# A two-layer hybrid-attention decoder: stick-breaking gates under their own units, the stick-breaking output projection under the softmax units, a later rotary factor, fewer gates at the end of attention

## The chip, the cores and the metric

The kernel runs on one core of a Trainium2 chip. The metric is the device time of one execution in microseconds (us). The engines are named as in the profile: PE (TensorE, matrix products), PEld (its weight loads), DVE (VectorE), ACT (ScalarE), POOL (GpSimd) and SP (SyncE, which issues most DMAs). Each engine works through its own instructions in order.

## The reference

Two layers over x of 512 rows and 1024 columns, all in float32:

```
h  = rms_norm(x, g_attn);  proj = h @ w_in              # 1024 -> 5120 columns
dq, dk, dv, sq, sk, sv, gates = split(proj)             # 6 x 512 columns and 2 x 1024
dq, dk = rope(dq), rope(dk)
o_diff = (softmax(q1 k1') - lam * softmax(q2 k2')) v    # 4 heads, then rms_norm over 128
o_sb:  a[i,j] = sigmoid(z[i,j]) * prod over j < t < i of sigmoid(-z[i,t]);  o = a v   # 8 heads of 64
g_diff, g_sb = split(sigmoid(gates + b_gate))
x = x + (g_diff * (o_diff @ w_o_diff) + g_sb * (o_sb @ w_o_sb)) @ w_out
x = x + (silu(gate) * up) @ w_ffn_out                   # gate, up = split(rms_norm(x, g_ffn) @ w_ffn_in)
```

and a last rms_norm. Hidden width of the FFN: 2816.

## The kernel before

Everything is kept transposed: a tile has 128 channels as partitions and the 512 rows of x as columns. Every large product is made of three matmuls: each float32 operand is split into a high part and a low part, and `mm_tiles` issues high x high, low x high and high x low for each of the eight (or four) blocks of 128 channels (lines 259 to 261). A group of 128 output channels is thus 24 matmuls of 128x512, or 12 where only half of the channels enter.

Weights come as a stream whose order is a list (`layer_order`). `w_pieces` allocates for entry n a raw buffer `wr` (three of them), a high part `wh` and a low part `wl` (four each), issues the DMA on SP, the cast `wr` to `wh` on ACT (L127) and the subtraction that gives `wl` on DVE, or on POOL for every fourth entry of w_in (L129). `w_get` hands the parts to the product and keeps the stream two entries ahead.

Attention has eight units: s0 to s3 are pairs of stick-breaking heads (class `SB`), d0 to d3 the softmax heads (class `Diff`). Each needs three groups of w_in (key, query, value). An SB unit makes scores, sigmoid (ACT, L504/506), a reverse scan (DVE), a product with the scan (POOL, L511), transposes on PE (L488), their high and low parts (`ths` on ACT L491, `tls` on DVE L492), and the map times values (`avs`, L522/523). A Diff unit makes scores, maxima, exponentials, a mix of two maps, transposes, `avd` (L576 to 578), squares `osd` and their parts `ohd`, `old` (L583 to 588), their mean `omd` on PE (L589/590), Ln and Exp (`rsqrt_of`, L206/207), three steps on DVE and the scaled output `od` (L592).

The order of the work on PE is set by a list of slots: while unit n runs, `fill` issues the three groups of unit n+1 and, from the fifth slot on, groups of gates (`FILL` is three groups in slots 0 to 3, four in 4 to 7). The 16 gates of a layer are w_in's groups 24 to 39, 24 to 31 for the softmax branch (`gd`) and 32 to 39 for the stick-breaking one (`gs`). Nine of them are left for the end (`TAIL0`). A gate's bank is multiplied by the norm's factor r on DVE; its sigmoid waits until the last Exp (`state["exp"]`), since ACT has to load another table for it. After attention, `parts` splits the eight unit outputs (L637); for each of the eight groups m of w_o, `ws` (stick-breaking half) and `wd` (softmax half) follow, then two sigmoids (L655, L656), three DVE operations that merge, and the split of the result. Then come the output projection `wo` and the FFN.

At the start of a layer the two halves of the rotary table `cs` are multiplied by r (L355, L356), ahead of the first evictions of unit s0 (`kns`, `qns`, `vns`, L397). `vns` feeds the transposes `vts` on PE (L450). `table()` loads the ACT tables: sigmoid for the SB units, Ln and Exp behind their last sigmoid.

The code before is written in program order; the framework's scheduler then orders each engine's instructions.

Of the kernel before, what the change touches and what calls it, by code (L numbers as in the profile page):

```python
# [34 lines left out]
BUFS = dict(mx=4, sm=4, blk=12, tmp=5, stk=6, v=3, wk=4, wT=3)  # L35
BANK_BUFS = dict(mm=3, at=5)
W_BUFS, W_AHEAD = 4, 2
GATES_IN_BLK = 4
# [6 lines left out]
FILL = (3, 3, 3, 3, 4, 4, 4, 4)  # L45
# [8 lines left out]
def trunk(ctx: ExitStack, tc, xT, par, tab, scn, msk, w_in, w_o, w_out, w_fi, w_fo, out):  # L54
# [17 lines left out]
    GATES = []  # L72
    for m in range(8):
        GATES += [("in", 24 + 8 + m), ("in", 24 + m)]
    layer_order = list(unit_groups(UNITS[0]))
    slots = []
    gi = 0
    for n in range(8):
        g = unit_groups(UNITS[n + 1]) if n < 7 else []
        while len(g) < FILL[n] and gi < len(GATES):  # L80
            g.append(GATES[gi])
            gi += 1
        slots.append(g)
# [28 lines left out]
    def w_pieces(*steps):  # L112
# [5 lines left out]
        raw = wp.tile([P, 1024], F32, name=f"wr{n}", tag="wr", bufs=3)  # L118
# [4 lines left out]
        for n_cols in steps:  # L123
# [4 lines left out]
            eng = nc.gpsimd if stream[n][1] == "in" and n % 4 == 0 else nc.vector  # L128
# [3 lines left out]
    def w_sums():  # L132
# [5 lines left out]
        pool, tag, bufs = (wp, "wr", 3) if j % 2 else (fp, "wx", 2)  # L138
# [133 lines left out]
    nrm = Norm(C_NA, "a0")  # L272
    pieces = [w_pieces(128, 384, 512), w_pieces(512, 512), w_pieces(1024)]
# [54 lines left out]
    for l in range(DEPTH):  # L328
        h = nrm.h
        with ExitStack() as ac:  # L330
# [24 lines left out]
            nc.vector.tensor_tensor(out=cs[:, 0], in0=cs[:, 0], in1=r, op=ALU.mult)  # L355
            nc.vector.tensor_tensor(out=cs[:, 1], in0=cs[:, 1], in1=r, op=ALU.mult)  # L356
# [8 lines left out]
            pair = [None]  # L365
            TAIL = list(TAIL0)

            def gate_group(key):
# [3 lines left out]
                n = len(gates)  # L372
                if n < GATES_IN_BLK:
                    t = blk(f"gt{j}")
                elif n < GATES_IN_BLK + BUFS["stk"]:
                    t = T("stk", f"gt{j}")
                elif n < GATES_IN_BLK + BUFS["stk"] + 2:
                    t = T(f"klz0{n - GATES_IN_BLK - BUFS['stk']}", f"gt{j}")
                else:
                    q = (n - GATES_IN_BLK - BUFS["stk"]) % 2  # L380
                    if q == 0:
                        pair[0] = T("wk", f"gt{j}", (P, 1280))
                    t = pair[0][:, q * S:q * S + S]
# [112 lines left out]
            class SB(Unit):  # L496
                def maps(self, c):
# [7 lines left out]
                    for i, (o, n) in enumerate(BANKS):  # L505
# [3 lines left out]
                    nc.vector.tensor_tensor_scan(out=e[:, ::-1], data0=e[:, ::-1], data1=msc[:, ::-1], initial=1.0,  # L509
                                                 op0=ALU.mult, op1=ALU.max)  # L510
# [3 lines left out]
                def mix(self, c, a):  # L514
# [9 lines left out]
                    if c == 0:  # L524
                        self.o = blk("o" + self.n)
# [11 lines left out]
            class Diff(Unit):  # L537
# [25 lines left out]
                def mix(self, m1, m2):  # L563
# [15 lines left out]
                    self.o = blk("o" + self.n)  # L579
# [27 lines left out]
            def fill(key):  # L607
                n = sum(u.done == 3 for u in units)
# [5 lines left out]
            for i in range(16 + LAG):  # L614
# [21 lines left out]
            def parts(t, hi, lo):  # L636
# [268 lines left out]
```

## Time and profile before

| | |
|---|---|
| median of 3 runs | 1497.26 us (1497.13 to 1498.28) |
| the profiled execution | 1496.57 us |
| its span | 1494.8 us |
| PE busy | 1461.4 us, 98% |
| DVE, ACT, POOL busy | 976.0, 691.8, 483.0 us |
| mean granted clock of PE | 0.995 |

The span is the time from the first to the last instruction in the trace; the time of an execution is a little longer. Busy time is summed by engine; engines run side by side. Matmul instructions overlap in the trace, so the distance of two starts and not the duration of one is what a matmul takes. A row of a timeline reads: start, duration, engine, line, operation, output<-inputs, shape, and in brackets the idle time just before with what ended it. Layer 0's attention lies at about 35 to 285 us, layer 1's at about 775 to 1030.

### The profile page before, as it was taken

How to read it: one execution, taken by the hardware profiler on the slowest of the kernel's cores; microseconds unless marked ns; L12 is line 12 of the kernel's file. 1: busy time of each engine (PE TensorE's matmuls, PEld its weight loads, DVE VectorE, ACT ScalarE, POOL GpSimd, SP SyncE). 2: the span in 40 equal slices, each digit the busy share in tenths (PEclk: the TensorE clock that was granted, in tenths of full speed). 3: DMA queues.
4: the chain of work that ended last, by engine and by line, in shares of the span. 5: the costliest groups of instructions: out<-in, count | busy, mean ns of one | idle time of the engine just before them, and what ended most of it. 6: DMA issues, size and time to landing. Idle time of an engine off the chain costs nothing.

```text
span 1494.8 us, 19780 instructions
## 1 busy us (share of the span) xinstructions
PE 1461.4 (98%) x7670; PEld 1253.0 (84%) x7670; DVE 976.0 (65%) x1229; ACT 691.8 (46%) x1122; POOL 483.0 (32%) x317
## 2 busy tenths in 40 slices
PE   9899999999999999999998999999999999999996
PEld 7788888888888998998886878888888989989885
DVE  6978776475765757654658777765648467477544
ACT  5656554643642433433444645546336334335342
POOL 2454652001140723530224455510022226155112
PEclk9999999999999999999999999999999999999998
DMA  7122232132323323223421122322323233232232
GB/s 254 46 78 69 75 102 86 57 124 94 106 96 103 108 87 105 90 83 87 134 85 57 64 75 88 100 81 80 103 94 117 90 99 113 74 124 71 87 88 66
DMA packets 45934, 139.73 MB, mean 93 GB/s; under 512 B 5904, under 2 KB 8336, under 8 KB 45840
## 3 DMA queue, kind: packets, MB, share of 16 engines
q1 hardware_dynamic: 45120, 137.91, 28.7%
q8 instruction: 60, 0.98, 0.3%
q10 hardware_dynamic: 720, 0.56, 0.1%
q14 instruction: 34, 0.28, 0.1%
HBM read 132.16 MB, written 2.10 MB: 90 GB/s over the span
## 4 chain that ended last, share of the span: by engine, by line
PE 87%; DVE 6%; ACT 3%; issue 1%; POOL 1%; DMA 1%; SPq 0%; DVEq 0%; POOLq 0%; ACTq 0%
PE fa L725 8%; PE fc L725 4%; PE pg L259 4%; PE pg L260 4%; PE pg L261 4%; PE fo L259 3%; PE fo L260 3%; PE fo L261 3%; PE fg L259 3%; PE fg L260 3%; PE fu L261 3%; PE fg L261 3%; PE fu L260 3%; PE fu L259 3%; PE fb L725 2%; PE wo L259 2%
## 5 line engine op out<-in xcount | busy, mean ns | idle before, releaser
L127 ACT CAST wh<-wr 128x1024 fp32r<-128x1024 f32 (+4 forms) x223 | 213.8, 964 | 327.5 <-issue 55.3
L129 DVE TENSOR_TENSOR wl<-wr,wh 128x1024 fp32r<-128x1024 f32 (+3 forms) x201 | 247.6, 1236 | 77.4 <-ACT wh L127 75.9
L259 PE MATMUL pg<-hha,wh 128*128 128x512 f32 x256 | 101.0, 394 | 0.0
L261 PE MATMUL pg<-hla,wh 128*128 128x512 f32 x256 | 100.3, 392 | 0.0
L260 PE MATMUL pg<-hha,wl 128*128 128x512 f32 x256 | 100.1, 391 | 0.0
L129 POOL TENSOR_TENSOR wl<-wr,wh 128x1024 fp32r<-128x1024 f32 (+3 forms) x22 | 50.7, 2305 | 111.8 <-ACT wh L127 99.2
L706 POOL TENSOR_TENSOR p<-u,g 128x512 f32<-128x512 f32 x22 | 34.4, 1563 | 158.0 <-DVE u L763 154.5
L242 POOL TENSOR_TENSOR accf<-accf,sqf 128x512 f32<-128x512 f32 x10 | 18.5, 1846 | 199.9 <-ACT sqf L240 199.9
L259 PE MATMUL fo<-ah,wh 128*128 128x512 f32 (+1 forms) x220 | 82.8, 376 | 0.0
L260 PE MATMUL fo<-ah,wl 128*128 128x512 f32 (+1 forms) x220 | 82.6, 375 | 0.0
L261 PE MATMUL fo<-al,wh 128*128 128x512 f32 (+1 forms) x220 | 82.3, 376 | 0.0
L259 PE MATMUL pd<-hha,wh 128*128 128x512 f32 x192 | 76.4, 398 | 0.3 <-ACT knd3s L404 0.3
L260 PE MATMUL pd<-hha,wl 128*128 128x512 f32 x192 | 76.2, 397 | 0.0
L261 PE MATMUL pd<-hla,wh 128*128 128x512 f32 x192 | 76.0, 396 | 0.0
L144 POOL TENSOR_TENSOR tf<-ru,rg 128x512 f32<-128x512 f32 x22 | 31.8, 1446 | 128.5 <-DMA ru<-in_w_fi_dram 112.3
L259 PE MATMUL fg<-hhf,wh 128*128 128x512 f32 x176 | 69.1, 393 | 0.0
L260 PE MATMUL fg<-hhf,wl 128*128 128x512 f32 x176 | 69.1, 393 | 0.0
L261 PE MATMUL fu<-hlf,wh 128*128 128x512 f32 x176 | 68.7, 390 | 0.0
L261 PE MATMUL fg<-hlf,wh 128*128 128x512 f32 x176 | 68.7, 390 | 0.0
L260 PE MATMUL fu<-hhf,wl 128*128 128x512 f32 x176 | 68.6, 390 | 0.0
L259 PE MATMUL fu<-hhf,wh 128*128 128x512 f32 x176 | 68.6, 390 | 0.0
L259 PE MATMUL ps<-hha,wh 128*128 128x512 f32 x144 | 58.8, 409 | 0.0
(452 smaller groups left out, 4492.0 us busy)
## 6 DMA issues: line engine op xcount, KB each, us to landing
wr<-in_w_in_dram SPq DMA_DIRECT2D x78, 512.0 KB, 3.3
wr<-in_w_fi_dram SPq DMA_DIRECT2D x44, 512.0 KB, 3.3
wr<-in_w_fo_dram SPq DMA_DIRECT2D x32, 384.0 KB, 3.1
rg<-in_w_fi_dram SPq DMA_DIRECT2D x22, 512.0 KB, 3.3
ru<-in_w_fi_dram SPq DMA_DIRECT2D x22, 512.0 KB, 3.3
wr<-in_w_fo_dram SPq DMA_DIRECT2D x32, 320.0 KB, 2.9
wr<-in_w_o_dram SPq DMA_DIRECT2D x16, 512.0 KB, 3.3
wr<-in_w_out_dram SPq DMA_DIRECT2D x16, 512.0 KB, 3.3
```

The costliest lines, as they stand in the source:

```text
L127: nc.scalar.copy(out=hi[:, c], in_=raw[:, c])
L129: state["wl"] = eng.tensor_tensor(out=lo[:, c], in0=raw[:, c], in1=f32(hi[:, c]), op=ALU.subtract)
L144: tt = lambda eng, o, a, b: eng.tensor_tensor(out=o, in0=a, in1=b, op=ALU.subtract)
L242: eng.tensor_tensor(out=self.acc, in0=self.acc, in1=sq, op=ALU.add)
L259: nc.tensor.matmul(dst, hi[:, c], rh, start=first and k == 0, stop=False)
L260: nc.tensor.matmul(dst, lo[:, c], rh, start=False, stop=False)
L261: nc.tensor.matmul(dst, hi[:, c], rl, start=False, stop=last and k == n - 1)
L706: (nc.vector if u.space == bass.MemoryType.PSUM else nc.gpsimd).tensor_tensor(out=p, in0=u, in1=g, op=ALU.mult)
L725: nc.tensor.matmul(dst, x[:, c], y, start=first and k + n == 0, stop=n == 2 and k == len(a) - 1, skip_group_check=True)
```

## The change

- Gates of the stick-breaking branch (`GS`): two in each of slots 0 to 3. They have buffers of their own (tag `gs`), and their sigmoids follow at once, with the table that the SB units use.
- Gates of the softmax branch (`GD`): one in slot 4, three in slot 7, four in the tail. Their eight sigmoids still wait for the last Exp.
- w_o is streamed in halves, `os` (stick-breaking) and `od` (softmax), 16 entries of 512 columns instead of 8 of 1024. The `os` groups run in slots 5 and 6, two in each, and four in the tail; `ws` times gate is formed there. The outputs of the SB units are split inside the units.
- After the last unit only the `od` groups are left, m = 0 and 1 first over the first three units.
- The two multiplications of `cs` come after the fourth scan.
- Raw weight buffers: two instead of three, and one of its own for the first entry. POOL no longer makes the low part of the entries 0, 4 and 132.

```diff
-GATES_IN_BLK = 4
-FILL = (3, 3, 3, 3, 4, 4, 4, 4)
...
+    GD, GS = [("in", 24 + m) for m in range(8)], [("in", 32 + m) for m in range(8)]
+    OS = [("os", m) for m in range(8)]
+    slots = [GS[0:2], GS[2:4], GS[4:6], GS[6:8], GD[0:1], OS[0:2], OS[2:4], GD[1:4]]
+    for n in range(7):
+        slots[n] = slots[n] + unit_groups(UNITS[n + 1]) if n == 3 else unit_groups(UNITS[n + 1]) + slots[n]
+    TAIL0 = [GD[4], OS[4], GD[5], GD[6], OS[5], GD[7], OS[6], OS[7]]
...
-    layer_order += [("o", m) for m in range(8)] + [("out", m) for m in range(8)]
+    layer_order += [("od", m) for m in range(8)] + [("out", m) for m in range(8)]
...
+        if kind in ("od", "os"):
+            return w_o[l, i][:, 512 * (kind == "os"):][:, :512]
...
-        raw = wp.tile([P, 1024], F32, name=f"wr{n}", tag="wr", bufs=3)
+        if n:
+            raw = wp.tile([P, 1024], F32, name=f"wr{n}", tag="wr", bufs=2)
+        else:
+            raw = state["w0"].tile([P, 1024], F32, name="wr0")
...
-            eng = nc.gpsimd if stream[n][1] == "in" and n % 4 == 0 else nc.vector
+            eng = nc.gpsimd if stream[n][1] == "in" and n % 4 == 0 and n % len(layer_order) > 6 else nc.vector
...
-            nc.vector.tensor_tensor(out=cs[:, 0], in0=cs[:, 0], in1=r, op=ALU.mult)
-            nc.vector.tensor_tensor(out=cs[:, 1], in0=cs[:, 1], in1=r, op=ALU.mult)
...
+            def os_group(m):
+
+                b = bank("mm", f"ws{m}_{l}")
+                hi, lo = w_get(l, "os", m)
+                mm_tiles(b, hi, lo, os_, True, True)
+                nc.vector.tensor_tensor(out=gates[8 + m], in0=b, in1=gates[8 + m], op=ALU.mult)
...
                 gates[j] = t
+                if j >= 8:
+                    bias = pt[:, C_BG + 16 * l + j:C_BG + 16 * l + j + 1]
+                    sigs.append(nc.scalar.activation(out=t, in_=t, func=AF.Sigmoid, bias=bias))
...
+                    if c == 1:
+                        os_.append(parts(self.o, T("osp", "oh" + self.n, dt=F32R), T("osp", "ol" + self.n, dt=F32R)))
...
+                    if i == 3:
+                        with tc.issue_after(state["z"].ins):
+                            for a in range(2):
+                                nc.vector.tensor_tensor(out=cs[:, a], in0=cs[:, a], in1=r, op=ALU.mult)
                     if i == 7:
-                        state["tab"] = table(LNEXP, state["sig"])
+                        with ExitStack() as order:
+                            for s in sigs:
+                                order.enter_context(tc.issue_after(s.ins))
+                            state["tab"] = table(LNEXP, state["sig"])
...
+            for u in units[4:]:
+                od_.append(parts(u.o, hp.tile([P, S], F32R, name=f"oh{u.n}_{l}", tag="hh"),
+                                 hp.tile([P, S], F32R, name=f"ol{u.n}_{l}", tag="hl")))
             merged = []
+
+            wd = [(fbank(f"wd{m}_{l}"),) + w_get(l, "od", m) for m in range(2)]
+            for b, hi, lo in wd:
+                mm_tiles(b, hi, lo, od_[:3], True, False)
             for m in range(8):
-                hi, lo = w_get(l, "o", m)
-                bs, bd = fbank(f"ws{m}_{l}"), fbank(f"wd{m}_{l}")
-                mm_tiles(bs, hi, lo, os_, True, True, 4)
-                mm_tiles(bd, hi, lo, od_, True, True, 0)
+                if m < 2:
+                    bd, hi, lo = wd[m]
+                    mm_tiles(bd, hi, lo, od_[3:], False, True, 3)
+                else:
+                    bd = fbank(f"wd{m}_{l}")
+                    mm(bd, (l, "od", m), od_)
...
                 with tc.issue_after(state["exp"].ins):
-                    nc.scalar.activation(out=gs, in_=gs, func=AF.Sigmoid, bias=pt[:, bg + 8 + m:bg + 9 + m])
                     sig = nc.scalar.activation(out=gd, in_=gd, func=AF.Sigmoid, bias=pt[:, bg + m:bg + 1 + m])
-                nc.vector.tensor_tensor(out=gs, in0=bs, in1=gs, op=ALU.mult)
                 nc.vector.tensor_tensor(out=gd, in0=bd, in1=gd, op=ALU.mult)
                 nc.vector.tensor_tensor(out=gd, in0=gd, in1=gs, op=ALU.add)
```

What the scheduler makes of it is shown at three places. First PE at the end of layer 0's attention, before: d3 is the last unit, `omd3` its mean square, `pg38` a gate's group (behind the second `omd3` follow nine more rows of it and three further gates of 24 rows, then the first `ws`).

```order
L260 MATMUL pg38_0_2622<-hha03_140,wl36_2559 128x512
L261 MATMUL pg38_0_2622<-hla03_141,wh36_2558 128x512
L589 MATMUL omd3_0_2508<-ohd3_0_2509,ones_v_79 128x512
L259 MATMUL pg38_0_2622<-hha04_148,wh36_2558 128x512
L260 MATMUL pg38_0_2622<-hha04_148,wl36_2559 128x512
L261 MATMUL pg38_0_2622<-hla04_149,wh36_2558 128x512
L590 MATMUL omd3_0_2508<-old3_0_2510,ones_v_79 128x512
L259 MATMUL pg38_0_2622<-hha05_156,wh36_2558 128x512
```

PE in the change, the same place: `ohd2`, `old2` are the parts of the third softmax unit's output, `ohd3_0_2954` the high part of the last one's, `wd0` to `wd3` groups of w_o's softmax half (13 `wd` rows between the two `omd3` rows are left out).

```order
L589 MATMUL avd3_0_2750<-thd3_0_2732,vd3_0_2324 128x128
L600 MATMUL omd3_0_2768<-ohd3_0_2769,ones_v_79 128x512
L258 MATMUL wd2_0_3008<-ohd0_0_2942,wh50_2960 128x512
L601 MATMUL omd3_0_2768<-old3_0_2770,ones_v_79 128x512
L260 MATMUL wd0_0_2958<-old2_0_2951,wh48_2904 128x512
L260 MATMUL wd1_0_2965<-old2_0_2951,wh49_2924 128x512
L260 MATMUL wd2_0_3008<-old2_0_2951,wh50_2960 128x512
L260 MATMUL wd3_0_3033<-old2_0_2951,wh51_2967 128x512
L258 MATMUL wd0_0_2958<-ohd3_0_2954,wh48_2904 128x512
L259 MATMUL wd0_0_2958<-ohd3_0_2954,wl48_2905 128x512
```

The gates that stood around and behind `omd3` are gone from there: 14 matmuls of `wd` lie between its two halves, four behind the second, and the next needs `ohd3_0_2954`.

ACT at the same place, in the change: `yod3` is the Ln and Exp of the last unit's mean square, `gt0` to `gt7` the softmax branch's gates (six of them left out).

```order
L205 ACTIVATE yod3_0_2775<-omd3_0_2768,eps_81 128x512
L206 ACTIVATE yod3_0_2775<-yod3_0_2775 128x512
L675 ACT_TABLE_LOAD
L675 ACTIVATE gt0_0_1856<-gt0_0_1856,pt_70 128x512
L675 ACTIVATE gt7_0_2900<-gt7_0_2900,pt_70 128x512
L267 ACT_TABLE_LOAD
L367 CAST ohd3_0_2954<-od3_0_2763 128x512
L126 CAST wh52_3010<-wr52_3009 128x512
L126 CAST wh53_3035<-wr53_3034 128x512
```

The cast of the last unit's output stands behind eight sigmoids and two table loads; before, it stood behind 15 sigmoids and one load, with 81 gate matmuls on PE meanwhile.

DVE at the start of layer 0's units, before and in the change:

```order
L210 SCALAR_TENSOR_TENSOR ya0_311<-ta0_312,ya0_311 128x512
L355 TENSOR_TENSOR cs_0_322<-cs_0_322,ya0_311 128x512
L356 TENSOR_TENSOR cs_0_322<-cs_0_322,ya0_311 128x512
L397 TENSOR_TENSOR kns0_0_334<-p00_0_197,ya0_311 128x512
L397 TENSOR_TENSOR qns0_0_344<-p01_0_198,ya0_311 128x512
```

```order
L209 SCALAR_TENSOR_TENSOR ya0_315<-ta0_316,ya0_315 128x512
L406 TENSOR_TENSOR kns0_0_336<-p00_0_201,ya0_315 128x512
L406 TENSOR_TENSOR qns0_0_346<-p01_0_202,ya0_315 128x512
L406 TENSOR_TENSOR vns0_0_354<-p02_0_203,ya0_315 128x512
L406 TENSOR_TENSOR kns1_0_422<-ps10_0_391,ya0_315 128x512
```

The two multiplications of `cs` have left this place, and the evictions of the first unit follow the norm's factor (`ya0`) at once.

## Rows read from the trace of the kernel before

**Rows 1.** The page: the span, and each engine's busy time.
```profile
span 1494.8 us, 19780 instructions
...
PE 1461.4 (98%) x7670; PEld 1253.0 (84%) x7670; DVE 976.0 (65%) x1229; ACT 691.8 (46%) x1122; POOL 483.0 (32%) x317
```
**Rows 2.** Stretches: length, busy time by engine, PE's granted clock, DMA.
```profile
35.00:60.00 25.00, 21.88 (x97) 17.68 (x96) 21.03 (x25) 14.91 (x24) 8.68 (x5) 0.93 0.26 85
60.00:80.00 20.00, 15.97 (x86) 13.15 (x85) 19.03 (x15) 11.40 (x22) 12.63 (x5) 1.00 0.07 26
80.00:120.00 40.00, 40.00 (x216) 33.90 (x214) 30.23 (x33) 24.77 (x47) 23.14 (x11) 1.00 0.23 73
120.00:160.00 40.00, 38.46 (x211) 32.66 (x211) 33.51 (x42) 22.74 (x45) 21.74 (x13) 1.00 0.22 63
160.00:200.00 40.00, 40.00 (x204) 33.95 (x203) 27.39 (x47) 22.93 (x50) 20.91 (x15) 1.00 0.33 104
...
780.00:815.00 35.00, 27.94 (x131) 22.22 (x130) 27.58 (x20) 18.82 (x37) 19.30 (x8) 0.95 0.14 45
...
860.00:920.00 60.00, 57.12 (x293) 47.08 (x292) 43.79 (x67) 31.30 (x64) 31.86 (x22) 1.00 0.26 80
920.00:1030.00 110.00, 110.00 (x542) 92.98 (x541) 70.23 (x110) 55.80 (x108) 36.99 (x24) 1.00 0.26 84
...
1030.00:1470.00 440.00, 440.00 (x2391) 383.38 (x2390) 270.62 (x328) 185.08 (x259) 117.46 (x80) 1.00 0.30 95
```
**Rows 3.** PE's waits in 30 to 300 and 750 to 1050: total, times, longest.
```profile
PE avs L523 <- DVE tls L492: 3.7, 3, 2.2
...
PE avs L523 <- DVE tls L492: 6.2, 4, 3.8
```
**Rows 4.** DVE's timeline at the first unit of layer 0.
```profile
39.61 2.87 DVE L356 TENSOR_TENSOR cs<-cs,ya 128x512 f32<-128x512 f32 x1
...
43.60 0.68 DVE L397 TENSOR_TENSOR vns<-p,ya 128x512 f32<-128x512 f32 x1
```
**Rows 5.** PE's timeline at the same place.
```profile
40.63 0.39 PE L260 MATMUL ps<-hha,wl 128*128 128x512 f32 x1
40.86 0.39 PE L261 MATMUL ps<-hla,wh 128*128 128x512 f32 x1
44.34 0.66 PE L450 MATMUL vts<-ident,vns 128*128 128x128 f32 x4 [3.09 <-DVE vns L397]
```
**Rows 6.** The page's groups: DVE's low parts of weights, total and mean ns.
```profile
L129 DVE TENSOR_TENSOR wl<-wr,wh 128x1024 fp32r<-128x1024 f32 (+3 forms) x201 | 247.6, 1236 | 77.4 <-ACT wh L127 75.9
```
**Rows 7.** PE's timeline at the end of layer 0's attention.
```profile
278.33 0.27 PE L578 MATMUL avd<-thd,vd 128*128 128x128 f32 x1
...
285.35 0.40 PE L590 MATMUL omd<-old,ones_v 128*128 128x512 f32 x1
```
**Rows 8.** ACT's timeline at the same place.
```profile
279.61 0.60 ACT L587 ACTIVATE ohd<-avd 128x512 fp32r<-128x512 f32 x1
...
285.78 0.69 ACT L206 ACTIVATE yod<-omd,eps 128x512 f32<-128x512 f32 x1 [2.83 <-PE omd L590]
286.50 0.63 ACT L207 ACTIVATE yod<-yod 128x512 f32<-128x512 f32 x1
287.15 1.28 ACT L655 ACT_TABLE_LOAD   x1
288.45 0.72 ACT L655 ACTIVATE gt<-gt,pt 128x512 f32<-128x512 f32 x1
289.08 0.71 ACT L656 ACTIVATE gt<-gt,pt 128x512 f32<-128x512 f32 x1
...
299.89 0.61 ACT L637 CAST ohs<-os 128x512 fp32r<-128x512 f32 x1
```
**Rows 9.** DVE's timeline, the scaled output of an earlier softmax unit.
```profile
245.25 0.75 DVE L592 SCALAR_TENSOR_TENSOR od<-ofd,gsub,yod 128x512 f32<-128x512 f32 x1
```
**Rows 10.** The page's DMA issues: count, size, median us from issue to landing.
```profile
wr<-in_w_fo_dram SPq DMA_DIRECT2D x32, 320.0 KB, 2.9
```

More of the change, by code (lines that the diff above doesn't have):

```diff
@@ L70, in unit_groups @@
         return [("in", c + i) for c in ((4, 0, 8) if kind == "d" else (16, 12, 20))]
-    GATES = []
-    for m in range(8):
-        GATES += [("in", 24 + 8 + m), ("in", 24 + m)]
-    layer_order = list(unit_groups(UNITS[0]))
[L76 to L83, printed above, removed]
+    GD, GS = [("in", 24 + m) for m in range(8)], [("in", 32 + m) for m in range(8)]
[4 more added lines that the diff above has]
+    TAIL0 = [GD[4], OS[4], GD[5], GD[6], OS[5], GD[7], OS[6], OS[7]]
+    layer_order = list(unit_groups(UNITS[0]))
+    for g in slots + [TAIL0]:
         layer_order += g
-    TAIL0 = GATES[gi:]
-    layer_order += TAIL0
-    layer_order += [("o", m) for m in range(8)] + [("out", m) for m in range(8)]
+    layer_order += [("od", m) for m in range(8)] + [("out", m) for m in range(8)]
     FFN = []
@@ L106, in w_src @@
             return w_fo[l, i][:, c0 * P:c1 * P]
-        return {"in": w_in, "o": w_o, "out": w_out, "fi": w_fi}[kind][l, i]
+        if kind in ("od", "os"):
+            return w_o[l, i][:, 512 * (kind == "os"):][:, :512]
+        return {"in": w_in, "out": w_out, "fi": w_fi}[kind][l, i]
     ready = []
@@ L137, in w_sums @@
         fp = state["fp"]
-        pool, tag, bufs = (wp, "wr", 3) if j % 2 else (fp, "wx", 2)
+        pool, tag, bufs = (wp, "wr", 2) if j % 2 else (fp, "wx", 2)
         rg = pool.tile([P, 2, 512], F32, name=f"rg{n}", tag=tag, bufs=bufs)
@@ L272, in trunk @@
     nrm = Norm(C_NA, "a0")
+    wctx = ExitStack()
+    state["w0"] = wctx.enter_context(tc.tile_pool(name="w0", bufs=1))
     pieces = [w_pieces(128, 384, 512), w_pieces(512, 512), w_pieces(1024)]
@@ L281, in trunk @@
             pass
+    wctx.close()
     after_h = state["hh"], state["hl"], state["wl"]
@@ L364, in trunk, with parts @@
             gates = {}
-            pair = [None]
+            sigs = []
+            os_, od_ = [], []
             TAIL = list(TAIL0)
+            def parts(t, hi, lo):
+                nc.scalar.copy(out=hi, in_=t)
+                nc.vector.tensor_tensor(out=lo, in0=t, in1=f32(hi), op=ALU.subtract)
+                return hi, lo
+            def os_group(m):
[3 more added lines that the diff above has]
+                nc.vector.tensor_tensor(out=gates[8 + m], in0=b, in1=gates[8 + m], op=ALU.mult)
             def gate_group(key):
@@ L371, in gate_group @@
                 j = key[1] - 24
[L372 to L375, printed above, removed]
+                if j >= 8:
+                    t = T("gs", f"gt{j}")
+                elif j == 0:
+                    t = T("os", f"gt{j}")
+                elif j < 7:
                     t = T("stk", f"gt{j}")
-                elif n < GATES_IN_BLK + BUFS["stk"] + 2:
-                    t = T(f"klz0{n - GATES_IN_BLK - BUFS['stk']}", f"gt{j}")
-                else:
[L380 to L383, printed above, removed]
+                else:
+                    t = T("wk", f"gt{j}", (P, 1280))[:, 0:S]
                 nc.vector.tensor_tensor(out=t, in0=b, in1=r, op=ALU.mult)
                 gates[j] = t
+                if j >= 8:
+                    bias = pt[:, C_BG + 16 * l + j:C_BG + 16 * l + j + 1]
+                    sigs.append(nc.scalar.activation(out=t, in_=t, func=AF.Sigmoid, bias=bias))
             class Unit:
@@ L524, in mix @@
                     if c == 0:
-                        self.o = blk("o" + self.n)
+                        self.o = T("os", "o" + self.n)
                     hs, ls = (slice(0, 64), slice(64, 128))[::1 - 2 * c]
@@ L578, in mix @@
                         nc.tensor.matmul(b[:, kb * P:], vl, hi[:, o:o + n], start=False, stop=kb == 3)
-                    self.o = blk("o" + self.n)
+                    self.o = T("od", "o" + self.n) if self.i < 2 else T(f"klz0{self.i - 2}", "o" + self.n)
                     o = tmp("of" + self.n)
@@ L607, in fill @@
             def fill(key):
+                if key[0] == "os":
+                    os_group(key[1])
+                    return
                 n = sum(u.done == 3 for u in units)
```

19 lines of the change are left out of this document (4 added, 15 removed).

## The prediction

> **What bounds the kernel now.** I read the page's busy shares first: PE is busy 1461.4 us of a span of 1494.8 [rows 1], so all its idle time together is 33.4 us, and since the change neither adds nor removes PE work worth counting (the halves of w_o make the same matmuls), it can gain only from those 33.4 us and from stretches at a lower clock. Then the table by stretches shows where the idle time is [rows 2]: in layer 0's attention 3.12 us in 35 to 60, 4.03 in 60 to 80, 1.54 in 120 to 160, together 8.7; in layer 1's 7.06 in 780 to 815 and 2.88 in 860 to 920, together 9.9. These are the stick-breaking units. Under the softmax units (920 to 1030), where gates already lie between the steps, PE idles for nothing. Third, the granted clock in the same rows: 0.93 over 25 us and 0.95 over 35 us, that is 0.07 x 25 and 0.05 x 35 = 1.75 us lost in each layer; each fall follows one of the layer's large waits, and in the other rows of that table the clock is 1.00. So at stake are 18.6 us of idle time and 3.5 of clock, 22.1 us. The waits' view says what ends most of the large waits: DVE's subtraction for the transposed maps, 3.7 us in layer 0 and 6.2 in layer 1 [rows 3].
>
> **What the change gains.** *The rotary factor.* At the start of layer 0, DVE makes two multiplications of cs ahead of the first unit's evictions, the second of 2.87 us [rows 4]; PE's wait for that eviction is 3.09 us [rows 5]. The two are moved behind the fourth scan. The eviction comes at least 2.87 us sooner, so I take 3.0 off, and with it layer 0's clock fall, which begins behind this gap: 3.0 + 1.75 = 4.75 us. The moved pair sits ahead of later stick-breaking subtractions, 0.7 us each where POOL is quiet; I count it inside the next term's uncertainty.
>
> *Gates under the stick-breaking units.* Eight gates of 24 matmuls go there in each layer. One matmul takes 0.227 us (40.63 to 40.86 in [rows 5]), so 8 x 24 x 0.227 = 43.6 us of PE work. What remains to be won is 8.7 - 3.0 + 9.9 of idle time plus layer 1's 1.75 of clock: 17.3 us. It isn't all won, since each gate also brings DVE a split of 1.24 us [rows 6] and a multiplication of 0.68 us (like the eviction in [rows 4]). From 35 to 160 DVE is busy 103.8 of 125 us, 83% [rows 2]; with 8 x 1.92 and four splits of the unit outputs (4 x 0.68) it is 121.9 of 168.6, 72%. At 68% (160 to 200) PE waits for nothing, at 79% (780 to 815) and 84% (120 to 160) it waits. 72% is nearer to the first, but PE takes its instructions in order, and a gate helps only where it stands in front of the late operation. Ends 0 and 17.3; I take two thirds, 11.5. Gains together: 16.3 us.
>
> **What the change costs: the end of attention, in each layer.** Before, the last softmax unit's chain (squares, omd, Ln, Exp, the scaled output, its cast) runs under PE work that needs none of it: behind the second omd matmul stand 9 + 72 = 81 matmuls of gates, 81 x 0.227 = 18.4 us. The order shows that of them nothing is left: the gates of this branch and the w_o groups come earlier, and behind the last avd matmul PE has 18 matmuls until it needs the cast of the last unit's output. On ACT that cast stands behind Ln, Exp, a table load, eight sigmoids and a second table load.
> 1. The first omd matmul now follows the last avd matmul at once and waits for ohd. Before, ohd was ready at 279.61 + 0.60 = 280.21, 1.88 us after the last avd matmul began [rows 7, 8]. That is 1.8 us of PE.
> 2. From the second omd matmul to PE's next possible work, by ACT's rows [rows 7, 8]: 0.43 until Ln begins, 0.72 to Exp, 0.65 to the table load, 1.30 to the first sigmoid, 8 x 0.63 = 5.04 for eight, 1.30 for the second load, 0.61 for the cast (the one at 299.89), 10.05 in all. PE has five matmuls meanwhile (omd and four of old2), 1.1 us. Starved: 9.0 us. DVE's four steps of the scaled output, 0.75 us each [rows 9], run beside the sigmoids and end before them.
> 3. A gap of this size is longer than those ahead of both clock falls, so I take one more fall: 1.75 us (ends 0 and two, 3.5).
> 4. The next halves (wd4 on) find their weights late: the hi part reuses a buffer that wd0 has just left, and the lo part on DVE stands behind two gate multiplications that wait for wd0 and wd1. Three DVE operations of about 0.65 us, against four or five matmuls: 1.0 us (0.8 to 1.2).
> 5. Raw buffers are two instead of three, so the load for wd7 starts only when wd5's lo part is made, some 6 us after the cast of item 2; 2.9 us to land for a piece of this kind [rows 10], and a cast. PE is at wd7 after 9.1 us (40 matmuls), the weight after 10. The same recurs at the second output group: 2.0 together (0, if the loads land as early as before, to 4).
> Sum 1.8 + 9.0 + 1.75 + 1.0 + 2.0 = 15.6 for a layer, 31.1 for two.
>
> Counted at nothing: the eight sigmoids brought under the stick-breaking units (0.63 each on an ACT that is busy 54 to 62% there [rows 2], and the sigmoid table is loaded there anyway); 16 more loads by SP and casts of halves (same bytes); the w_o groups' multiplications, under softmax units where DVE is busy 64% [rows 2]; three lo parts moved from POOL to DVE. If DVE's slack at the softmax units went, these would show as waits for subtractions there.
>
> **Sum.** 31.1 - 16.3 = +14.8 us. The profiled execution took 1496.57 us, so 1511.4; the median of the runs is 0.7 above it: **1512**. The costs' low end is what ACT's order alone enforces, 2 x (1.8 + 9.0) = 21.6; with all 22.1 gained this gives 1496.8. The high end, 2 x (1.8 + 9.0 + 3.5 + 1.2 + 4.0) = 39.0 with 4.75 gained, gives 1531.5.
>
> **The rivals.**
> *The gates don't fill the waits* (the change doesn't do what it says): the late subtractions stay late, since the added work stands behind them in PE's order. For it: at 95% DVE share (60 to 80) more DVE work can only push subtractions back. Against: share falls over the stretch. Gain 4.75 only: 1524. Chance 0.13.
> *The two sides cancel*: all waits under the stick-breaking units go and items 3 to 5 come to nothing: 1496.8 + 0.7 = 1497.5, no change. For it: 72% is near 68%. Against: three terms must all be off the same way. Chance 0.10. (What a measurement can tell from no change is about 0.2%, 3 us.)
> *Faster: busy PE hides a stall.* In the stick-breaking stretch the short transposes and map products may each be held a little by the semaphores between PE and DVE without showing as idle, and gates between them would take that away. From 35 to 160 PE does 610 instructions in 116.3 us, 0.191 each; with 0.02 us less on each, two layers give 24 us: 1512 - 24 = 1488. It decides from 0.015 on, where it outweighs the net loss by 3 us. Against: 160 to 200, with gates between, shows 0.196 each, no less. Chance 0.10.
> *The ring of two raw buffers starves the FFN too*: 64 pieces of its second product at 0.25 us each, 16 us: 1528. Against: in layer 1's output and FFN (1030 to 1470) PE is busy 440.00 of 440 us [rows 2], so the weights are there well before PE now. Chance 0.04.
> *Switching tables costs more than its load.* In the trace the load starts 0.02 us after Exp has ended (286.50 + 0.63) and the sigmoid 0.02 us after the load [rows 8]; nothing else is paid. If a pause of one load's length, 1.28 us, stood at each of the two switches now on the path, that would be 2.6 us a layer: 1517. Chance 0.03.
> The Trainium skill, in "ScalarE: Activation LUTs", section "What ACT_TABLE_LOAD costs", gives some 1283 ns for a load, and that page of the Trainium skill counts about 2.7 us for a switch with its drain. The load agrees with this trace; the drain does not show in it. By the whole price of the Trainium skill, item 2 would be some 2.8 us longer in each layer, an estimate.
>
> **How the numbers follow.** The forecast has the remaining 0.60. Its own spread (gain by 6 either way, costs by 6) is 1503 to 1521. To hold 8 in 10 the range takes in the cancelling case's lower half and the unfilled waits: **1495 to 1526**. Faster by over 0.2%: the hidden stall and a little of the cancelling case's edge, 0.12; same: 0.10; slower: 0.78.
>
> **What the profile after would show.** Right: idle time on PE of 8 to 10 us behind omd in each layer, ended by ACT's cast of the last unit's output, with two table loads and eight sigmoids just ahead of it; a clock fall right after; PE idle under the stick-breaking units a third of 18.6 us or less; no 3 us wait for the first eviction. Wrong: a cast of that output ahead of the sigmoids, PE idle under 5 us there, or a stick-breaking stretch shorter by more than its 18.6 us of idle time and its clock loss once the 43.6 us are taken off.

## The result, and the profile after

The changed kernel takes 1530.68 us (median of four runs, 1529.38 to 1532.55), the kernel before 1497.53 beside it: ratio 1.0216, 95% interval 1.0204 to 1.0228. It is slower, as forecast, but by more than twice the forecast amount, and the time lies above the range.

The page after, the lines that answer to [rows 1]:

```profile
span 1527.6 us, 19807 instructions
...
PE 1471.2 (96%) x7670; PEld 1256.5 (82%) x7670; DVE 977.7 (64%) x1251; ACT 693.0 (45%) x1138; POOL 472.9 (31%) x311
```

The span grew by 32.8 us: PE's idle time from 33.4 to 56.4 us, and 9.8 us more PE time for the same 7670 instructions. Where it lies is seen in the stretches (length, busy time of PE, PEld, DVE, ACT and POOL, granted clock, DMA):

```profile
36.00:60.00 24.00, 23.10 (x118) 19.36 (x116) 21.12 (x24) 16.64 (x30) 11.10 (x6) 1.00 0.18 60
60.00:80.00 20.00, 17.16 (x75) 13.79 (x76) 19.86 (x16) 9.56 (x18) 8.26 (x3) 0.91 0.23 79
...
250.00:300.00 50.00, 47.81 (x232) 39.81 (x231) 34.26 (x58) 20.70 (x44) 15.93 (x11) 1.00 0.24 80
...
327.50:362.00 34.50, 22.82 (x87) 17.23 (x86) 21.19 (x34) 19.33 (x30) 0.00 (x0) 0.85 0.13 46
...
405.00:761.00 356.00, 353.24 (x1986) 310.07 (x1985) 220.35 (x263) 146.68 (x208) 108.84 (x75) 1.00 0.31 97
...
800.00:850.00 50.00, 47.05 (x239) 39.26 (x238) 37.39 (x32) 24.24 (x44) 19.92 (x8) 1.00 0.22 74
...
1075.00:1113.00 38.00, 24.81 (x91) 18.73 (x89) 21.47 (x34) 19.43 (x30) 0.00 (x0) 0.82 0.14 42
...
1157.00:1514.00 357.00, 354.32 (x2047) 313.34 (x2045) 213.04 (x258) 145.93 (x210) 108.23 (x75) 1.00 0.29 91
```

Under the stick-breaking units the idle time fell, from 8.7 to 3.7 us in layer 0 and from 9.9 to 3.0 in layer 1 (compare [rows 2]). At the end of attention, where PE did not idle before, it now idles for 11.7 and 13.2 us at a lowered clock. And both FFNs idle, for 2.8 and 2.7 us; before, layer 1's lay in a stretch of 440 busy us of 440 ([rows 2]), and layer 0's had no idle time either:

```profile
391.00:743.00 352.00, 352.00 (x1986) 309.76 (x1985) 221.82 (x263) 146.92 (x208) 108.99 (x75) 1.00 0.31 98
```

PE's waits after (total, times, longest), from three stretches:

```profile
PE ss L482 <- DVE vs L470: 2.1, 1, 2.1
...
PE wd L258 <- ACT ohd L367: 8.8, 1, 8.8
PE omd L600 <- ACT ohd L598: 1.7, 1, 1.7
PE ws L258 <- DVE gt L376: 1.1, 1, 1.1
...
PE fa L743 <- ACT a L758: 1.9, 2, 1.6
PE fc L743 <- DVE tal L149: 0.6, 1, 0.6
```

The end of layer 0's attention, on ACT and then PE's next matmul, answers to [rows 8]:

```profile
333.47 0.69 ACT L205 ACTIVATE yod<-omd,eps 128x512 f32<-128x512 f32 x1 [3.50 <-PE omd L601]
334.19 0.63 ACT L206 ACTIVATE yod<-yod 128x512 f32<-128x512 f32 x1
334.83 1.28 ACT L675 ACT_TABLE_LOAD   x1
336.13 5.00 ACT L675 ACTIVATE gt<-gt,pt 128x512 f32<-128x512 f32 x8
341.15 1.28 ACT L267 ACT_TABLE_LOAD   x1
342.44 0.62 ACT L367 CAST ohd<-od 128x512 fp32r<-128x512 f32 x1
```

```profile
343.12 0.80 PE L258 MATMUL wd<-ohd,wh 128*128 128x512 f32 x1 [8.78 <-ACT ohd L367]
...
345.84 0.63 PE L258 MATMUL wd<-ohd,wh 128*128 128x512 f32 x1
346.27 0.63 PE L259 MATMUL wd<-ohd,wl 128*128 128x512 f32 x1
```

Ln, Exp, load, eight sigmoids, load, cast, then PE: the chain of the prediction, 8.78 us where it said 9.0. Behind the gap two matmuls start 0.43 us apart instead of 0.23: the granted clock is 0.50 from 344 to 348, the lower of its two levels.

A table by PE's own starts (first product of a layer, last avd, first output group wo, first FFN group, end of the FFN's last product) splits the 32.8 us:

| stretch | before | after | difference |
|---|---|---|---|
| layer 0, first product to last avd | 273.3 | 322.6 | +49.3 |
| last avd to first wo | 69.1 | 33.4 | -35.7 |
| output groups | 43.5 | 44.0 | +0.5 |
| FFN | 351.5 | 355.5 | +4.0 |
| layer 1, first product to last avd | 271.4 | 314.5 | +43.2 |
| last avd to first wo | 70.3 | 36.3 | -33.9 |
| output groups | 43.5 | 45.2 | +1.7 |
| FFN | 353.0 | 357.0 | +3.9 |

Work moves across the last avd: behind it stood 304 and 309 matmuls, and now 80 and 86, so 224 x 0.227 = 50.8 us and 223 x 0.227 = 50.6 changed sides. Without that, the part up to the last avd gained 50.8 - 49.3 = 1.5 us in layer 0 and 7.4 in layer 1; the end of attention lost 15.1 and 16.7, the output 0.5 and 1.7, the FFNs 7.9.

### The profile page after: what moved, and what is told of

It reads as the page before. It is cut to its first block, busy times and chain, and to the rows that moved or that the text cites. A ratio compares the mean times of both kernels' runs of the same rounds, so it can differ in the third digit from the quotient of the medians.

```text
span 1527.6 us, 19807 instructions
## 1 busy us (share of the span) xinstructions
PE 1471.2 (96%) x7670; PEld 1256.5 (82%) x7670; DVE 977.7 (64%) x1251; ACT 693.0 (45%) x1138; POOL 472.9 (31%) x311
## 4 chain that ended last, share of the span: by engine, by line
PE 78%; DVE 8%; ACT 4%; DMA 4%; POOL 3%; issue 3%; SPq 0%; DVEq 0%; POOLq 0%; ACTq 0%
PE fa L743 6%; PE fc L743 3%; PE pg L258 3%; PE pg L260 3%; PE pg L259 3%; PE pd L258 3%; PE pd L259 3%; PE pd L260 3%; PE fg L258 2%; PE fg L259 2%; PE fg L260 2%; PE fu L260 2%; PE fu L259 2%; PE fu L258 2%; POOL tf L143 2%
## 5 line engine op out<-in xcount | busy, mean ns | idle before, releaser
L126 ACT CAST wh<-wr 128x1024 fp32r<-128x1024 f32 (+4 forms) x239 | 217.1, 913 | 313.5 <-PE pg L260 38.8
L128 DVE TENSOR_TENSOR wl<-wr,wh 128x1024 fp32r<-128x1024 f32 (+4 forms) x223 | 260.4, 1171 | 109.5 <-ACT wh L126 108.7
L724 POOL TENSOR_TENSOR p<-u,g 128x512 f32<-128x512 f32 x22 | 30.4, 1382 | 150.2 <-DVE u L781 150.2
L259 PE MATMUL fg<-hhf,wl 128*128 128x512 f32 x176 | 69.1, 393 | 0.0
L520 POOL TENSOR_TENSOR zs<-zs,es 128x1279 f32<-128x1279 f32 x16 | 43.5, 2721 | 80.4 <-DVE es L518 77.5
L518 DVE TENSOR_TENSOR_SCAN es<-es,msc 128x1280 f32<-128x1280 f32 x16 | 50.0, 3128 | 14.5 <-ACT es L513 14.5
```

The lines of the kernel that those rows point to most:

```text
L126: nc.scalar.copy(out=hi[:, c], in_=raw[:, c])
L128: state["wl"] = eng.tensor_tensor(out=lo[:, c], in0=raw[:, c], in1=f32(hi[:, c]), op=ALU.subtract)
L259: nc.tensor.matmul(dst, lo[:, c], rh, start=False, stop=False)
L518: state["z"] = nc.vector.tensor_tensor_scan(out=e[:, ::-1], data0=e[:, ::-1], data1=msc[:, ::-1], initial=1.0, op0=ALU.mult, op1=ALU.max)
L520: nc.gpsimd.tensor_tensor(out=z[:, 0:1279], in0=z[:, 0:1279], in1=e[:, 1:1280], op=ALU.mult)
L724: (nc.vector if u.space == bass.MemoryType.PSUM else nc.gpsimd).tensor_tensor(out=p, in0=u, in1=g, op=ALU.mult)
```

## The experiments

Different runs stood on different chips, so each time is compared by its ratio to the kernel before on the same chip, whose median was 1497.85 in the first four runs, 1499.06 in the next four, then 1498.36 and 1498.76.

### Two raw buffers or three

Run one puts the ring of two into the kernel before:

```diff
-        raw = wp.tile([P, 1024], F32, name=f"wr{n}", tag="wr", bufs=3)
+        raw = wp.tile([P, 1024], F32, name=f"wr{n}", tag="wr", bufs=2)
...
-        pool, tag, bufs = (wp, "wr", 3) if j % 2 else (fp, "wx", 2)
+        pool, tag, bufs = (wp, "wr", 2) if j % 2 else (fp, "wx", 2)
```

> The kernel before with two raw weight buffers instead of three, nothing else. Theory (the ring is what the FFN lost in the change: 4.0 and 3.9 us between first fg and the end of the FFN): the same 8 us appear here, about 1505.5 us, with PE waits fa <- ACT a of 1.6 us and fc <- DVE tal of 0.6 in each layer. Rival (the FFN's loss comes from the new order of instructions, not from the ring): no change, 1497.5 within 1.5.

Run two puts three into the change:

```diff
+            raw = wp.tile([P, 1024], F32, name=f"wr{n}", tag="wr", bufs=3)
...
+        pool, tag, bufs = (wp, "wr", 3) if j % 2 else (fp, "wx", 2)
...
-                    self.o = T("od", "o" + self.n) if self.i < 2 else T(f"klz0{self.i - 2}", "o" + self.n)
+                    self.o = rp.tile([P, S], F32, name=f"o{self.n}_{l}", tag=("sq", "acc")[self.i], bufs=1) if self.i < 2 else T(f"klz0{self.i - 2}", "o" + self.n)
```

> The changed kernel with three raw buffers again (room is made by putting two softmax outputs into buffers of the norm that are idle during attention). Theory: FFN stretches back to 351.5 and 353.0 us (8 us less), and most of the late weights at the end of attention gone (waits of 0.8, 0.3 and 0.2 us in layer 0, 1.4 and 1.4 in layer 1), 3 to 4 us: 1519 to 1520 us. The wait for the cast of the last output stays at 8.8. Rival (order, not ring): 1530.7 within 2.

Run one took 1515.47 us, ratio 1.0119 (1.0104 to 1.0134); run two 1522.83, ratio 1.0165 (1.0148 to 1.0182). The FFN stretches decide it, of the kernel before with two buffers and then of the change with three:

```profile
401.50:757.00 355.50, 352.47 (x1982) 309.40 (x1981) 220.41 (x262) 146.42 (x207) 109.10 (x75) 1.00 0.31 97
1142.50:1501.40 358.90, 355.45 (x2046) 314.71 (x2045) 212.25 (x257) 146.32 (x210) 108.49 (x75) 1.00 0.29 90
```

```profile
411.50:763.00 351.50, 351.50 (x1983) 309.39 (x1982) 220.87 (x262) 146.60 (x207) 108.78 (x75) 1.00 0.32 98
1154.00:1507.10 353.10, 353.10 (x2047) 313.15 (x2046) 213.61 (x257) 146.59 (x210) 108.72 (x75) 1.00 0.29 90
```

With three buffers PE idles nowhere in the FFNs, which take 351.5 and 353.0 us as before; with two, also in the old order, it idles for 3.0 and 3.4, and they take 4.3 and 5.9 us longer. The FFN loss is the ring's, shown both ways. In the change's layer 0 the chain ahead of fa's wait (1.62 us, until 615.55) names the path: a buffer free late, its load, three differences on POOL, a cast on ACT and a subtraction on DVE; then the next round of differences, which needs the buffer `tf` that the subtractions leave. The cast of one of them stands on ACT ahead of the small copy `a` for which PE waits:

```profile
597.71 3.57 DMA ru<-in_w_fi_dram
...
601.44 1.27 POOL tf L143
```

```profile
614.18 1.04 ACT L148 CAST whh<-ru 128x1024 fp32r<-128x1024 f32 x1 [4.70 <-POOL ru L143]
615.13 0.37 ACT L758 COPY a<-fa 128x256 f32<-128x256 f32 x1
```

Both totals missed. Run one lost 10 us more in layer 0's attention, where it lacks the first entry's own buffer that the change has (the second unit's first product starts 4.0 us later); that this buffer is the reason was not tested. Run two lost 7.0 in layer 0 up to the first output group (a wait of 4.0 for the subtraction of a map, 3.0 ahead of the first transposes), while in layer 1 attention and output gained 5.1. What happens at layer 0's start changed with these edits in ways that were not forecast, and this recurs below.

### The rotary factor alone

The edit is the change's own: the two multiplications leave their place and follow the fourth scan, in the kernel before.

> The kernel before with only the two multiplications of the rotary table moved behind the fourth scan. Theory as predicted: the first wait (3.09 us) and layer 0's clock fall go, 4.75 us: 1492.8. Rival, after the changed kernel's trace (a wait of 2.1 us for the first unit's values and the clock fall later in layer 0): the time only moves to the next late DVE operation, and to the moved pair itself, 1496 to 1498.

1497.12 us against 1497.85, ratio 0.9994 (0.9984 to 1.0003): nothing. PE in three stretches (compare [rows 2]), and two of its waits:

```profile
35.00:60.00 25.00, 25.00 (x126) 21.00 (x125) 22.52 (x25) 17.96 (x31) 10.04 (x6) 1.00 0.26 85
60.00:80.00 20.00, 15.95 (x75) 13.19 (x74) 15.43 (x15) 10.81 (x19) 13.23 (x6) 0.91 0.13 34
80.00:160.00 80.00, 75.50 (x403) 62.35 (x403) 66.37 (x76) 45.45 (x88) 41.70 (x22) 1.00 0.22 67
```

```profile
72.88 0.59 PE L521 MATMUL avs<-tls,vs 128*128 128x512 f32 x1 [2.47 <-DVE tls L490]
...
118.56 0.50 PE L471 MATMUL ss<-kas,qas 128*128 128x512 f32 x1 [2.27 <-DVE vs L459]
```

The 3.09 us of [rows 5] are gone: PE does not idle from 35 to 60. But from 80 to 160 it idles for 4.5 us instead of 1.5 (2.27 of them for a later unit's values), so that 35 to 160 holds 8.6 us of idle time after 8.7 before, and the clock fall has only moved, from the first row into the second. The rival holds.

### What stands ahead of the cast

Run four orders the sigmoids behind the cast (`cast3`, the high part of the last unit's output); run five makes them without another table (`nbg` holds the negated biases, `one` a column of ones):

```diff
-                with tc.issue_after(state["exp"].ins):
+                with tc.issue_after(cast3.ins):
                     sig = nc.scalar.activation(out=gd, in_=gd, func=AF.Sigmoid, bias=pt[:, bg + m:bg + 1 + m])
```

> The changed kernel with its eight softmax-gate sigmoids ordered behind the cast of the last unit's output instead of behind the last Exp. Theory A (ACT's order holds whatever stands behind the sigmoids): the cast's wait falls from 8.8 to about 4.2 us, but now the weight cast for wd4 stands behind two loads and eight sigmoids, 7.6 + 0.6 us after the cast against 2.7 us of matmuls, a new wait of 5 to 5.5: time within 2 us of 1530.7. Theory B (only the place of that one cast matters): 4.6 us less in each layer, 1521.5.

```diff
+                else:
+                    with tc.issue_after(state["tab"].ins):
+                        nc.scalar.activation(out=t, in_=t, func=AF.Exp, scale=-1.0, bias=nbg[:, 16 * l + j:16 * l + j + 1])
+                        nc.scalar.activation(out=t, in_=t, func=AF.Ln, bias=one[:, 0:1])
+                        nc.scalar.activation(out=t, in_=t, func=AF.Exp, scale=-1.0)
...
-                with tc.issue_after(state["exp"].ins):
-                    sig = nc.scalar.activation(out=gd, in_=gd, func=AF.Sigmoid, bias=pt[:, bg + m:bg + 1 + m])
...
-            table(LNEXP, sig)
```

> The changed kernel with the softmax branch's eight sigmoids made of Exp, Ln and Exp in the table that the softmax units use, right after each gate: no sigmoid and no table load is left at the end of attention. Theory (ACT's queue of loads and sigmoids holds the cast and, in the run with the cast first, the weights): the cast's wait falls from 8.8 to about 4.1 us and no weight wait of 3 us takes its place: below the run with the cast first (1524.5) by its waits of 3.6 and 2.8, 1517 to 1519. Rival: the 16 more ACT operations in each layer (10 us) delay the softmax units' exponentials and the time stays at 1524 or above.

Run four: 1524.51 us, ratio 1.0177 (1.0162 to 1.0193). Run five: 1524.06, ratio 1.0166 (1.0151 to 1.0181). Waits at the end of layer 0 in run four, then of layer 1 in run five:

```profile
PE wd L258 <- ACT ohd L367: 4.1, 1, 4.1
PE wd L258 <- ACT wh L126: 3.6, 1, 3.6
```

```profile
PE wd L262 <- ACT ohd L371: 4.1, 1, 4.1
PE wo L262 <- ACT wh L126: 2.6, 1, 2.6
```

The cast's wait fell from 8.8 to 4.1 as worked out, and as theory A has it, a good part came back as a wait for the weights behind the sigmoids, 3.6 us in layer 0 and 2.8 in layer 1 where I had put 5 to 5.5; the time, about 6 us less, lies between the two theories. In run five that wait is down to 1.1 and none, but in layer 1 the weights of the output came late (2.6 us; the run of eight gates with three buffers below has no such wait), and in both layers together the part up to the last avd took 2.5 us longer than in run four, which is the rival's side. So it gave nothing further, and my 1517 to 1519 overlooked the ring.

### How many gates under the stick-breaking units

Four runs share three raw buffers and the Exp and Ln form; only the table of slots differs (and, for the gates made after the sigmoid table is gone, their form). Eight as in the change; four:

```diff
+    slots = [GS[0:1], GS[1:2], GS[2:3], GS[3:4], GS[4:5], GS[5:6], [GS[6], OS[0]], [GS[7], GD[0], GD[1]]]
+    TAIL0 = [OS[1], GD[2], OS[2], OS[3], GD[3], OS[4], OS[5], GD[4], OS[6], OS[7], GD[5], GD[6], GD[7]]
```

none, with slots 0 to 3 empty and all 16 gates and the w_o groups from slot 4 on; and later five, with GS[0:2], GS[2:3], GS[3:4], GS[4:5] in slots 0 to 3. The table gives, from the profiled executions, each layer's stretch from its first product to its first FFN group; the ratio of five is against 1498.76.

> The same with three raw weight buffers: eight gates under the stick-breaking units, none left behind the last unit. Theory: 8 us less by the FFN and 2 to 3 by weights at the end: 1507 to 1510. Still left at the end of attention in each layer: 1.7 us for omd, 4.1 for the cast, a clock fall.

> The same with only four gates under the stick-breaking units, one in a slot; the others follow under the softmax units, and by the order 69 to 72 gate matmuls stand behind omd again. Theory (the end's wait is missing cover; the stick-breaking waits shrink with the work put there): no PE wait for the last cast and no clock fall there, 2 x (1.7 + 4.1 + 1.75) = 15 us less than with eight, and about half of the 12 us that eight gates saved there come back: about 1499. Rival (the end is bound by something other than cover): the wait for the last cast stays at 3 us or more.

> The same with no gate under the stick-breaking units, all 16 and the w_o groups under the softmax units and behind them. Theory: the waits under the stick-breaking units are those of the kernel before with the late rotary factor (about 9 and 9 us and a clock fall in each layer), the end waits for nothing: 1496 to 1499, the same as the kernel before. If it is below 1494, the Exp and Ln form or the split of w_o gains something of its own; if above 1501, they cost.

| gates there | time, us | ratio (interval) | layer 0 | layer 1 |
|---|---|---|---|---|
| kernel before | 1499.06 | 1 | 386.0 | 385.1 |
| none | 1508.80 | 1.0061 (1.0045 to 1.0077) | 394.0 | 386.0 |
| four | 1497.82 | 0.9993 (0.9983 to 1.0002) | 391.0 | 382.0 |
| five | 1491.90 | 0.9957 (0.9943 to 0.9970) | 388.9 | 376.5 |
| eight | 1515.34 | 1.0101 (1.0084 to 1.0119) | 402.1 | 387.4 |

In layer 0 all four are behind the kernel before, also with no gate moved; why its start became longer was not separated. Layer 1 shows the trade without that start: gates under the stick-breaking units pay up to the point where the last unit has no cover. With four the end of attention is free of waits (the stretches of the ends of layer 0 and 1), with eight it is not:

```profile
311.00:353.00 42.00, 42.00 (x190) 34.92 (x189) 29.86 (x45) 22.56 (x36) 0.00 (x0) 1.00 0.33 105
...
1047.00:1087.00 40.00, 40.00 (x181) 33.33 (x181) 29.11 (x45) 22.52 (x35) 0.00 (x0) 1.00 0.33 106
```

```profile
334.00:366.00 32.00, 25.60 (x98) 19.80 (x97) 22.18 (x34) 12.54 (x20) 0.00 (x0) 0.89 0.23 75
1071.00:1103.00 32.00, 25.64 (x97) 20.08 (x96) 20.21 (x32) 11.29 (x18) 0.00 (x0) 0.84 0.19 59
```

The rival for four (bound by something other than cover) falls. That its 1497.8 met the 1499 expected is in part luck, for the eight gates that it was counted from took 1515 and not 1507 to 1510. With none, 1508.8 against 1496 to 1499, most of the excess is layer 0's: PE waits 5.7 us for a unit's values there, and the layer takes 8 us more than before up to the FFN. With eight, layer 0 took 4.2 us more than in run five, half of that excess or more. In layer 1, none and the kernel before are 0.9 us apart (386.0 and 385.1): there the Exp and Ln form and the split of w_o cost little. Neither the split nor the low parts that POOL gave up was run by itself.

### The norm's mean, and the best version

The wait of 2.6 us for the first transposes came back in these runs, and the mean of the norm stood late in PE's order. Two runs put it ahead of most of the second unit's query and value groups:

```diff
+                        if l == 0 and which > 0 and (self.kind, self.i) == UNITS[1]:
+                            hi, lo = w_get(l, *key)
+                            k0 = 3 if which == 1 else 0
+                            if k0:
+                                mm_tiles(b, hi, lo, h[:k0], True, False)
+                            with tc.issue_after(state["ms"].ins):
+                                mm_tiles(b, hi, lo, h[k0:], k0 == 0, True, k0)
```

> The kernel before with the late rotary factor and the norm's mean taken earlier by PE in layer 0: it stands behind 33 instead of 39 or more matmuls of the second unit, so that Ln and Exp follow the last square. Theory (layer 0's units start with DVE late by a chain that begins with the norm's mean, so taking only the rotary pair out of it moved the wait): the mean comes about 3 us earlier, and the waits from 40 to 80 us fall from 8 to about 5: 1493 to 1495. Rival (the stretch is bound by DVE's own work, 95% busy from 60 to 80): the time stays within 1.5 us of 1497.

> The run with four gates under the stick-breaking units (1497.8) with the same early mean in layer 0. Theory: the wait of 2.6 us for the first transposes goes and the clock fall behind it: 1493 to 1495, faster than both kernels. Rival: 1497 to 1498, the wait moves on.

The first took 1501.12, ratio 1.0021 (1.0011 to 1.0031), a little slower, which neither theory nor rival had, with a new wait of 5.2 us for a unit's values; the second 1498.40, ratio 1.0000 (0.9991 to 1.0009). Again the wait moved, as the rival has it. Two more with five gates:

> The same with five gates under the stick-breaking units, two of them in the first slot. Theory: 1 to 1.5 us less waiting under the stick-breaking units in each layer than with four, and the end still covered (48 gate matmuls behind the last avd): 1491 to 1494. Rival (by order the cover just falls short or DVE is the bound): 1495 or more.

> Five gates under the stick-breaking units as in the 1485.7 us run, but with the norm's mean where the scheduler puts it, as with four gates at 1497.8. Theory (the gain is the fifth gate's: fewer waits and one clock fall less, the mean's place is worth nothing): 1485 to 1488. Rival (five gates gain only together with the early mean): 1492 to 1497.

With the early mean 1485.74, ratio 0.9918 (0.9905 to 0.9932), **faster than both kernels** and below the 1491 to 1494 expected; without it 1491.90, at the edge of the rival's 1492 to 1497 and not the theory's 1485 to 1488. So the fifth gate gains by itself, and the mean's place counts in layer 0 together with it (5 us; layer 1 is the same in both). Why it counts with five gates and hardly with four was not tried further. Stretches with four gates (early mean), then with five:

```profile
780.00:815.00 35.00, 30.83 (x146) 25.28 (x145) 28.90 (x23) 21.38 (x41) 18.48 (x8) 0.95 0.24 76
815.00:860.00 45.00, 43.43 (x217) 36.53 (x216) 34.82 (x32) 20.86 (x41) 14.63 (x6) 0.96 0.19 59
```

```profile
780.00:815.00 35.00, 35.00 (x179) 29.75 (x178) 27.48 (x25) 20.43 (x36) 18.88 (x8) 1.00 0.23 76
815.00:860.00 45.00, 45.00 (x241) 38.61 (x240) 32.21 (x35) 25.32 (x48) 14.89 (x7) 1.00 0.21 71
```

5.7 us of idle time and 0.05 x 35 + 0.04 x 45 = 3.6 of clock went with one gate more (layer 1 starts 5.3 us earlier in the second run, so the stretches are not quite the same work). Part of it came back from 860 to 930: 2.8 us of idle time against 0.9, and a clock of 0.98. In all layer 1 became 5.8 us shorter up to the FFN.

## Why the prediction was right and wrong

- *The end of attention*: right. Predicted for a layer 1.8 for omd, 9.0 for the cast, 1.75 of clock, 1.0 and 2.0 for weights, 15.6 in all; measured 15.1 + 0.5 in layer 0 and 16.7 + 1.7 in layer 1. The two large waits were 1.67 and 8.78. The clock took a little more: ten matmuls in layer 0 and thirteen in layer 1 started 0.43 us apart instead of 0.23, which is 2.0 and 2.6 us; in layer 1 it fell twice. For the weights PE waited 1.3 and 2.8 us where items 4 and 5 had 3.0. Runs four and five, which take the sigmoids from ahead of the cast, and the run of four gates, which puts the cover back, show that this chain is the cause.
- *"Raw buffers ... 2.0"* and the rival *"The ring of two raw buffers starves the FFN too"*, chance 0.04: this step failed. I took a PE that never waits as proof of slack; it says only that three buffers are enough, not that two are, and so the sum has the FFNs at nothing. The FFNs lost 7.9 us, half of the 16 that the rival was priced at (in each FFN PE waits at four places, not at every piece), and runs one and two show that the ring alone makes them.
- *"The rotary factor ... 4.75 us"*: failed. I followed one wait to its DVE operation without asking what PE waits for next. Alone it is worth nothing that can be measured (run three), and in the change the clock fall stayed (0.91 from 60 to 80). Nor were the 2.87 us of [rows 4] the multiplication's own: most of it was waiting for POOL, as the last section shows, and at its new place the pair waits again, 5.70 us for the two in layer 1 where I had put 0.7 each with POOL quiet.
- *"Gates under the stick-breaking units ... two thirds"*: near in size for layer 1 (7.4 against two thirds of 9.9 + 1.75 = 7.8), in part by luck: 6.9 us of idle time and the clock fall went, and 2.3 us of new waits (950 to 1050) were not counted. But layer 0 gained 1.5 in all where the two terms promised 8.5. There 5.0 us of idle time went, no clock came back, and 2.2 us of new waits came under the softmax units' w_o groups (250 to 300), which I had counted at nothing: PE waits there for a bank that DVE or ACT has not yet emptied (1.1 us for DVE's product of ws and gate), a group of 12 matmuls being short. Of the 7.0 us that are missing, these waits are 2.2, the clock 1.75 and idle time that stayed 1.8; the other 1.3 were not found. Why idle time and clock fall stayed in layer 0 and not in layer 1 is open. DVE's share, from which I took the two thirds, does not decide it: in the kernel before PE waits for nothing at 76% (80 to 120 in [rows 2]), and in the change it waits at 75% (800 to 850).
- *Sum*: gains 8.9 instead of 16.3, costs 34.0 + 7.9 instead of 31.1. Of the 18.0 us between forecast and result, 7.9 are the FFNs, 7.0 layer 0's gain, 0.4 layer 1's and 2.9 the ends. One slip beside it: the 1496.8 of the low end already holds the 0.7 between profiled execution and median, and the cancelling rival's 1497.5 adds it again.
- *The signs named*: the gap, the cast that ends it and the clock fall behind it came, and the first 3 us wait went. The idle time under the stick-breaking units, 6.7 of 18.6 us, is just over the third that was named.

## What to carry to other kernels

Filler work has to be counted at both ends: what is moved into a gap is taken from the place that it covered, so find the chain behind the last unit, work out its length, and leave that much behind it (here, of none, four, five and eight gates moved forward, five was best; six and seven were not tried). A stream that never makes its consumer wait tells nothing of what one buffer less would do: follow the load, the cast and what POOL and DVE still do with it. And a wait at the head of a stretch in which one engine is nearly always busy is worth nothing until the next late operation on that engine is known.

## What the runs showed of the hardware

DVE operations with two inputs from SBUF stand still while POOL works. In the change, DVE from 57 to 71 us and layer 1's moved pair of cs, and POOL in the first of these times:

```profile
57.29 3.46 DVE L128 TENSOR_TENSOR wl<-wr,wh 128x1024 fp32r<-128x1024 f32 x1
...
61.61 2.81 DVE L518 TENSOR_TENSOR_SCAN es<-es,msc 128x1280 f32<-128x1280 f32 x1
64.34 1.19 DVE L128 TENSOR_TENSOR wl<-wr,wh 128x1024 fp32r<-128x1024 f32 x1
65.46 5.07 DVE L518 TENSOR_TENSOR_SCAN es<-es,msc 128x1280 f32<-128x1280 f32 x1
...
843.53 5.70 DVE L639 TENSOR_TENSOR cs<-cs,ya 128x512 f32<-128x512 f32 x2
```

```profile
57.22 2.45 POOL L520 TENSOR_TENSOR zs<-zs,es 128x1279 f32<-128x1279 f32 x1 [2.85 <-DVE es L518]
64.56 3.28 POOL L520 TENSOR_TENSOR zs<-zs,es 128x1279 f32<-128x1279 f32 x1 [4.89 <-DVE es L518]
```

The subtraction takes 3.46 us when it starts behind POOL's product, and 1.19 when it starts 0.22 us ahead of it; that product then takes 3.28 instead of 2.45. The scan takes 2.81 alone and 5.07 behind POOL. The slow subtraction ends 1.08 us after POOL's operation (60.75 against 59.67), the slow scan 2.69 (70.53 against 67.84): about a whole operation behind, not a slower one. The Trainium skill says so in "SBUF — State Buffer", section "SBUF: two separate sides": whichever starts first, a GpSimd operation or a DVE operation with two inputs from SBUF, holds the shared ports for its whole instruction, and the trace agrees.

The same explains the 2.87 us of [rows 4]. Before, on DVE and then on POOL:

```profile
39.00 0.69 DVE L355 TENSOR_TENSOR cs<-cs,ya 128x512 f32<-128x512 f32 x1
```

```profile
39.18 2.76 POOL L129 TENSOR_TENSOR wl<-wr,wh 128x1024 fp32r<-128x1024 f32 x1 [12.81 <-ACT wh L127]
```

The first multiplication starts ahead of POOL's subtraction and takes 0.69 us; the second, of the same size, ends 0.54 us after it (42.48 against 41.94). The evictions are not held: in the change the first unit's, which read a PSUM bank, take 0.68 us each (39.37 to 41.84) beside a POOL subtraction from 39.00 to 41.41.

So DVE's 95% from 60 to 80 in [rows 2] held waiting for POOL too, and the split that a gate brings costs there not 1.24 but up to 3.5 us. Whether this made layer 0's small gain is not shown: no run took POOL out of the stretch, and POOL's share is the same where layer 1 gained more (8.26 us of 20 from 60 to 80, 19.92 of 50 from 800 to 850).
